# The opening of a hybrid decoder layer: x feature by token in three groups, rms by sums over partitions, gate sums moved into it

## The chip, the cores and the metric

One core of one Trainium2 chip. The metric is the device time of one execution in microseconds, the median of the runs; lower is better. A profile is one execution recorded by the hardware profiler.

## What is computed

One layer of a decoder on 1024 prompt tokens and 8 x 8 sample tokens (1088 tokens of 1024 features). The part that the change touches is the start: modulation by a condition, rmsnorm and the input projection.

```python
shift, scale, gate = jnp.split(jax.nn.silu(c) @ ada_w[l] + ada_b[l], 3, axis=-1)
h = rmsnorm(x, norm_w[l]) * (1.0 + scale[:, None, :]) + shift[:, None, :]
q_lat, kv_lat, k_pe, g_a, u, g_b, m_a, m_b = split_in(h @ w_in[l])
...
x = x + gate[:, None, :] * (merged @ w_out[l])

def rmsnorm(x, w):
    y = xf * lax.rsqrt(jnp.mean(xf * xf, axis=-1, keepdims=True) + EPS)
    return y.astype(x.dtype) * w
```

There is one condition for the prompt and one for each of the eight samples, so nine rows of shift, scale and gate. The rest (latent attention, a gated recurrence, two output projections, the final norm) is left as it is.

## The kernel before

All products are made of two parts: `split` (L53) casts a value to a high half on ACT (L55) and subtracts it on VectorE for the low half (L56); `mm3` (L76) issues three products, high x high, low x high and high x low (L79 to L81). The 1024 features lie in eight blocks (k) of 128 partitions; the tokens lie in three groups `GRP` of 364, 362 and 362 columns, of which the third ends with the 64 sample tokens.

The opening (L151 to L305) has these steps. `x_load` brings x in nine tiles of 128 tokens by 1024 features. `x_norm` (L220) squares a tile on ACT with a sum along its row, takes the power -0.5 on POOL (`rms_pow`, L109) and scales the tile on VectorE or POOL. `x_turn` (L231) turns it with eight transpositions on TensorE and copies it from PSUM to `xT`. `ada_load` (L184) brings block k of the shift and scale weights, 1 MB; `ada_sum` (L189) multiplies it by silu(c) on TensorE (eight fp32 products, in four strips of 32 partitions), and ACT copies the sum to `sa`; `ada_turn` (L199) transposes `sa` on TensorE, and VectorE adds the strips and writes block k of `aff`, the factors and shifts by feature. `h_part` (L241) applies them to the block on POOL (L245; the sample tokens on VectorE) and splits the result into `hh[k]` and `hl[k]`. `u_part` (L257) adds block k of the first two tiles of the u projection for one group: three products for each tile. The loop over k does for each block group 0 (six products), the turn of block k+1 and its `h_part` for all three groups, group 1, the sum of block k+2, and group 2.

Behind the opening comes `dense` (L372), the rest of the input projection: 26 tiles of 24 steps (`project`, L314, three products each), among which the sample attention and the recurrence are laid. Beside its tiles 2 to 17 runs `gate_sums` (L326): a load of 256 KB, four fp32 products with silu(c), and a VectorE copy or addition into `sgs`, which the end of the kernel reads as the gate.

TensorE's order is that of the program text (`manual_schedule` at L151). The other engines and SP's queue of DMAs get theirs from a planner, by the program's order as a priority, by when it takes an operand to be ready and by when a buffer of a pool comes free. Buffers of the opening's pool `p1`: three of `aw`; PSUM: four banks `pj`, two `pt` (both for the u sums) and two `px`.

Of the kernel before, what the change touches and what calls it, by code (L numbers as in the profile page):

```python
# [9 lines left out]
F32 = mybir.dt.float32  # L10
# [33 lines left out]
def trunk_step(ctx: ExitStack, tc: tile.TileContext, a, o):  # L44
# [76 lines left out]
    with ExitStack() as px_:  # L121
# [29 lines left out]
        with ExitStack() as pb, tc.manual_schedule(engines={mybir.EngineType.PE}):  # L151
# [30 lines left out]
            xT = p1.tile([P, KC, N], F32, name="xT", bufs=1)  # L182
# [6 lines left out]
            def ada_sum(aw):  # L189
# [5 lines left out]
                sa = p1.tile([P, 256], F32, name="sa")  # L195
# [13 lines left out]
            xs = {}  # L209

            def x_load(i):
                n = P if i < 8 else NS
                if i == 6:
                    xs[6] = p1.tile([P, KC, 256], F32, name="aw", bufs=3).rearrange("p a b -> p (a b)")
                    xs[6], xs[7] = xs[6][:, :D], xs[6][:, D:]
                elif i != 7:
                    xs[i] = p1.tile([P, D], F32, name="x", bufs=6)
                nc.sync.dma_start(xs[i][:n], a["xp"][i * P:(i + 1) * P] if i < 8 else a["xs"])

            def x_norm(i):  # L220

                n, x = P if i < 8 else NS, xs[i]
                st = p1.tile([P, 4], F32, name="st", bufs=4)
                S.activation(L[3][:n, :D], x[:n], AF.Square, accum_out=st[:n, 0:1])
                rms_pow(st[:n, 2:3], st[:n, 0:1], D, st[:n, 1:2])
                if i % 2:
                    G.tensor_scalar(x[:n], x[:n], st[:n, 2:3], 0.0, OP.mult, OP.add)
                else:
                    V.tensor_scalar(x[:n], x[:n], st[:n, 2:3], None, OP.mult)

            def x_turn(i):  # L231

                n, x = P if i < 8 else NS, xs[i]
                for j in range(2):
                    ps, tag = ((pt, "pt"), (pj, "pj"), (pj, "pj"))[(2 * i + j) % 3]
                    ps = ps.tile([P, 4, P], F32, name="pxt", tag=tag)
                    for k in range(4):
                        T.transpose(ps[:, k, :n], x[:n, (4 * j + k) * P:(4 * j + k + 1) * P], ident[:n, :n])
                    (S.copy if j == 0 and i % 2 == 0 else V.tensor_copy)(xT[:, 4 * j:4 * j + 4, i * P:i * P + n], ps[:, :, :n])

            def h_part(k, s, n):  # L241

                h = L[2 + k % 2][:, :N]
                m = min(s + n, NP)
                G.tensor_scalar(h[:, s:m], xT[:, k, s:m], aff[:, k, 1, 0:1], aff[:, k, 0, 0:1], OP.mult, OP.add)  # L245
                if s + n > NP:
                    h3 = hs[:, k].rearrange("p (b t) -> p b t", b=NB)
                    V.tensor_tensor(h3, xT[:, k, NP:].rearrange("p (b t) -> p b t", b=NB),
                                    aff[:, k, 1, 1:9].rearrange("p b -> p b ()").to_broadcast((P, NB, NT)), OP.mult)
                    V.tensor_tensor(h3, h3, aff[:, k, 0, 1:9].rearrange("p b -> p b ()").to_broadcast((P, NB, NT)),  # L250
                                    OP.add)
                    split(hh[k][:, NP:], hl[k][:, NP:], hs[:, k])
                split(hh[k][:, s:m], hl[k][:, s:m], h[:, s:m])
# [3 lines left out]
            def u_part(k, c, g):  # L257
                s, n = GRP[g]
                if k == 0:
                    pu[c, g] = (pj if g < 2 else pt).tile([P, 512], F32, name=f"pu{c}{g}", tag="pj" if g < 2 else "pt")  # L260
                mm3(pu[c, g][:, :n], [w[:, k, :] for w in u01[c]], [hh[k][:, s:s + n], hl[k][:, s:s + n]],
                    k == 0, k == KC - 1)

            for i in range(8):
                x_load(i)
            for i in range(9):
                x_norm(i)
                x_turn(i)
                if i == 0:
                    x_load(8)  # L270
                if i == 2:
                    aw = ada_load(0)
                if i == 3:
                    u01 = [weights(a["w_in"][c], (0,), (w_u0, None)[c]) for c in range(2)]
                    aw1 = ada_load(1)
                if i == 5:
                    sa = ada_sum(aw)
                if i == 6:
                    ada_turn(0, sa)
            aw = ada_load(2)  # L280
            h_part(0, *GRP[0])
            h_part(0, *GRP[1])
            h_part(0, *GRP[2])
            sa = ada_sum(aw1)
            for k in range(KC):
                if 0 < k and k + 2 < KC:
                    aw = ada_load(k + 2)
# [1131 lines left out]
```

## Time and profile before

| | us |
|---|---|
| median of 3 runs | 972.44 (972.28 to 972.62) |
| the profiled execution | 971.41 |
| its span, first to last instruction | 969.6 |
| busy: PE (TensorE matmul) | 936.1 (97%) |
| busy: DVE (VectorE) | 645.5 (67%) |
| busy: ACT (ScalarE) | 492.2 (51%) |
| busy: POOL (GpSimd) | 241.0 (25%) |

How to read the rows below. Times are us from the start of the span. A row of the timeline has start, duration, engine, line, operation, output and inputs, shapes, count (equal neighbours are merged into one row, from the first start to the last end) and in brackets how long the engine had been idle and what released it. PE is TensorE's products, PEld its weight loads. Matmuls are pipelined: their durations overlap, and the distance of two starts is what one costs. A row of the windows has the stretch, its length, the busy time of PE, PEld, DVE, ACT and POOL in it with the number of instructions, the granted TensorE clock (1.00 is 2.4 GHz), the share of the DMA engines, and GB/s. A row of the groups by form has line, engine, operation, tensors, shapes and count, then the busy time, the mean ns of one, and the idle time ahead of them. A row of one line's view has the shortest, median and longest duration in ns.

### The profile page before, as it was taken

To read this page: it belongs to the slowest core of one execution; us is meant where nothing else is said; L and a number is where in the kernel's file an instruction comes from. 1 tells how busy PE (TensorE), PEld (TensorE's weight loads), DVE (VectorE), ACT (ScalarE), POOL (GpSimd) and SP (SyncE) were. 2 spreads that over 40 slices of the span, in tenths; PEclk is the share of its full clock that TensorE was granted. 3 is DMA by queue.
4 is the path that set the end of the run, shared out by engine and by line. 5 is a ranking of instruction groups with operands and counts; after the bars stand their busy time and mean duration, and the time that the engine had idled before them with its cause. 6 is when DMAs were issued, how large, how long until landed. Compare 5 with 4: busy or idle time off the path is not lost. (4 is left out here: it accounts for less than half of the span.)

```text
span 969.6 us, 16493 instructions
## 1 busy us (share of the span) xinstructions
PE 936.1 (97%) x5933; PEld 860.2 (89%) x5933; DVE 645.5 (67%) x1518; ACT 492.2 (51%) x1150; POOL 241.0 (25%) x313
## 2 busy tenths in 40 slices
PE   5899999999999999999999999999999899999997
PEld 4677999999999999999999898888888799998886
DVE  5775664566666777766654367889889785880833
ACT  6447555544445444544443336777687664650311
POOL 5452210332222322222100034444445200000101
PEclk9999999999999999999999999999999999999999
DMA  9843132453443323333422213000011264741421
GB/s 337 287 142 110 49 108 94 146 152 109 141 129 125 113 77 120 103 110 119 117 78 97 65 53 69 12 7 22 7 34 34 69 198 155 246 140 35 152 87 66
DMA packets 52099, 104.62 MB, mean 108 GB/s; under 512 B 8177, under 2 KB 23601, under 8 KB 50994
## 3 DMA queue, kind: packets, MB, share of 16 engines
q1 hardware_dynamic: 46626, 84.69, 26.8%
q0 software_dynamic: 5392, 18.88, 6.6%
q8 instruction: 47, 0.77, 0.3%
q14 instruction: 34, 0.28, 0.1%
HBM read 85.58 MB, written 16.92 MB: 106 GB/s over the span
## 5 line engine op out<-in xcount | busy, mean ns | idle before, releaser
L79 PE MATMUL pj<-hh,whi 128*128 128x362 f32 (+2 forms) x656 | 223.9, 341 | 1.1 <-ACT L L145 1.1
L81 PE MATMUL pj<-hh,wlo 128*128 128x362 f32 (+2 forms) x656 | 217.1, 331 | 0.0
L80 PE MATMUL pj<-hl,whi 128*128 128x362 f32 (+2 forms) x656 | 216.8, 330 | 0.0
L79 PEld LDWEIGHTS pj<-hh,whi 128*128 128x128 f32 x656 | 123.5, 188 | 7.5 <-issue 4.7
L80 PEld LDWEIGHTS pj<-hl,whi 128*128 128x128 f32 x656 | 123.7, 189 | 1.7 <-issue 0.4
L81 PEld LDWEIGHTS pj<-hh,wlo 128*128 128x128 f32 x656 | 123.4, 188 | 1.7 <-issue 0.4
L644 POOL TENSOR_SCALAR nat<-raw 128x1024 fp32r<-128x1024 f32 x32 | 37.0, 1157 | 136.6 <-PE spo L65 81.6
L1038 POOL TENSOR_SCALAR pr<-pr,mx 128x128 f32<-128x128 f32 (+3 forms) x64 | 50.0, 782 | 83.2 <-DVE mx L1037 69.3
L1036 ACT ACTIVATE pr<-pr,mx 128x128 f32<-128x128 f32 (+3 forms) x64 | 49.8, 778 | 12.9 <-DVE mx L1034 12.6
L645 DVE TENSOR_TENSOR nat<-raw,nat 128x1024 fp32r<-128x1024 f32 x32 | 39.0, 1220 | 20.6 <-POOL nat L644 20.6
L641 POOL DMA_INDIRECT raw<-cache_ckv,idx x32 | 33.6, 1049 | 74.9 <-PE ptt L69 44.4
L1052 PE MATMUL ptr<-ident,pr 128*128 128x128 f32 x288 | 45.6, 276 | 4.1 <-DVE ptl L56 2.7
L112 POOL TENSOR_SCALAR ost<-ost 128x1 f32<-128x1 f32 (+1 forms) x9 | 2.9, 324 | 186.0 <-DVE ost L1296 186.0
L1293 ACT ACTIVATE ot<-xo 128x512 f32<-128x512 f32 (+2 forms) x19 | 11.5, 606 | 72.8 <-DVE xo L1292 68.5
L56 DVE TENSOR_TENSOR ptl<-ptr,pth 128x512 fp32r<-128x512 f32 (+1 forms) x80 | 45.7, 577 | 3.6 <-ACT pth L55 2.4
L694 ACT COPY stmp<-pss 64x512 f32<-64x512 f32 (+1 forms) x40 | 19.9, 497 | 55.0 <-PE pss L65 54.7
L56 DVE TENSOR_TENSOR wlo<-wraw,whi 128x512 fp32r<-128x512 f32 x58 | 39.4, 703 | 10.1 <-ACT whi L55 10.0
L55 ACT CAST pth<-ptr 128x512 fp32r<-128x512 f32 (+1 forms) x80 | 39.6, 499 | 9.7 <-PE ptr L1052 9.1
L56 DVE TENSOR_TENSOR tt<-ptt,tt 128x512 fp32r<-128x512 f32 x64 | 41.2, 679 | 4.8 <-ACT tt L55 4.4
L1052 PEld LDWEIGHTS ptr<-ident,pr 128*128 128x128 f32 x288 | 33.0, 140 | 12.6 <-DVE ptl L56 3.9
L55 ACT CAST whi<-wraw 128x512 fp32r<-128x512 f32 x58 | 34.0, 621 | 13.5 <-PE pj L80 13.4
L345 DVE COPY ev<-pj 128x364 f32<-128x364 f32 (+1 forms) x40 | 21.2, 530 | 29.4 <-PE pj L81 28.9
(472 smaller groups left out, 2588.5 us busy)
## 6 DMA issues: line engine op xcount, KB each, us to landing
wraw<-w_in SPq DMA_DIRECT2D x60, 256.0 KB, 3.2
sg<-g_dram SPq DMA_DIRECT2D x16, 544.0 KB, 3.6
aw<-ada_ss SPq DMA_DIRECT2D x8, 1024.0 KB, 7.2
g_dram<-ev SPq DMA_DIRECT2D x40, 181.0 KB, 2.4
wraw<-ada_g SPq DMA_DIRECT2D x16, 256.0 KB, 3.0
oraw<-w_out SPq DMA_DIRECT2D x16, 256.0 KB, 3.2
xo<-xp SPq DMA_DIRECT2D x8, 512.0 KB, 5.3
out_y<-xo SPq DMA_DIRECT2D x16, 256.0 KB, 2.1
```

The source lines that it names most:

```text
L55: S.copy(hi, src)
L56: V.tensor_tensor(lo, src, f(hi), OP.subtract)
L79: T.matmul(out, lhs[0], rhs[0], start=start, stop=False)
L80: T.matmul(out, lhs[0], rhs[1], start=False, stop=False)
L81: T.matmul(out, lhs[1], rhs[0], start=False, stop=stop)
L345: (S.copy if g == 1 else V.tensor_copy)(ev[:, :n], ps[:, :n])
L641: nc.gpsimd.indirect_dma_start(raw.rearrange("p k r -> p (k r)"), None, ckv_rows, bass.IndirectOffsetOnAxis(ap=idx[:, j, b:b + 1], axis=0))
L644: G.tensor_scalar(nat[:, 0], raw, 1.0, 0.0, OP.mult, OP.add)
L645: V.tensor_tensor(nat[:, 1], raw, f(nat[:, 0]), OP.subtract)
L1036: S.activation(pr[:, :w], pr[:, :w], AF.Exp, bias=mx[:, 1:2], scale=-1.0, accum_out=mx[:, 2:3])
L1038: G.tensor_scalar(pr[:, :w], pr[:, :w], mx[:, 3:4], 0.0, OP.mult, OP.add)
L1052: T.transpose(ps[:, k, i, :], pr[i][:, kc * P:(kc + 1) * P], ident)
```

## The change

x now comes transposed from the host, as three tensors of 128 partitions by 8 blocks by the group's tokens, two loads for each. The squares of a group are taken block by block on ACT and added on VectorE (`x_squares`); three narrow fp32 products with ones sum them over the partitions, so that a token lies on a partition, POOL takes the power, and VectorE writes three diagonal matrices (`x_rms`); one fp32 product with a 128 x 128 of ones spreads them, and ACT copies the result, R, one factor for each token on all partitions (`x_spread`). `h_part` multiplies a block by R on VectorE in place and then goes on as before; the sample tokens are done for all blocks at once (`h_sample`). The order of the opening is new: three blocks of group 0 first, then for each k the sum of block k+3, group 1 of block k, the turn of block k+3 and group 0 of block k+3; group 2 at the end. The gate's weights are laid out as four further blocks of 1 MB; their sums stand among the products of group 2 and are written by `ada_sum` to `sgs`, and `gate_sums` is gone from the dense loop.

```diff
-        G.tensor_tensor(out, tmp, nhalf[:n], OP.pow)
+        G.tensor_tensor(out, tmp, nhalf[:n].to_broadcast(tuple(out.shape)), OP.pow)
...
             def ada_load(k):
-                aw = p1.tile([P, KC, 256], F32, name="aw", bufs=3)
-                nc.sync.dma_start(aw, a["ada_ss"][k])
+                aw = p1.tile([P, KC, 256], F32, name="aw", bufs=4)
+                nc.sync.dma_start(aw, a["ada_ss"][k] if k < KC else a["ada_g"][k - KC])
                 return aw
...
+            def x_load(g):
                 for j in range(2):
+                    nc.sync.dma_start(xg[g][:, 4 * j:4 * j + 4], a[f"xT{g}"][:, 4 * j:4 * j + 4])
+
+            def x_squares(g):
+
+                n = GRP[g][1]
+                acc = p1.tile([P, 364], F32, name="acc", bufs=1)
+                S.activation(acc[:, :n], xg[g][:, 0], AF.Square)
+                for k in range(1, KC):
+                    sq = p1.tile([P, 364], F32, name="sq", bufs=2)
+                    S.activation(sq[:, :n], xg[g][:, k], AF.Square)
+                    V.tensor_tensor(acc[:, :n], acc[:, :n], sq[:, :n], OP.add)
+                return acc
+
+            def x_rms(g, acc):
...
+                for i in range(3):
+                    m = min(P, n - i * P)
+                    T.matmul(ps[:m, i:i + 1], acc[:, i * P:i * P + m], ones[:, 0:1], start=True, stop=True)
...
+                rms_pow(st[:, 4:7], st[:, 0:3], D, st[:, 0:3])
+                for i in range(3):
+                    V.tensor_scalar(rinv[:, i], ident, st[:, 4 + i:5 + i], None, OP.mult)
+
+            def x_spread(g):
+                n = GRP[g][1]
+                ps = px.tile([P, 512], F32, name="prb", tag="px")
+                T.matmul(ps[:, :n], ones, rinv.rearrange("p i t -> p (i t)")[:, :n], start=True, stop=True)
+                R[g] = p1.tile([P, 364], F32, name=f"R{g}", bufs=1)
+                S.copy(R[g][:, :n], ps[:, :n])
+
+            def h_part(k, g):
...
+                x = xg[g][:, k, :m - s]
+                V.tensor_tensor(x, x, R[g][:, :m - s], OP.mult)
+                G.tensor_scalar(h[:, s:m], x, aff[:, k, 1, 0:1], aff[:, k, 0, 0:1], OP.mult, OP.add)
+                split(hh[k][:, s:m], hl[k][:, s:m], h[:, s:m])
+
+            def h_sample():
+
+                m = NP - GRP[2][0]
+                V.tensor_tensor(hs, xg[2][:, :, m:], R[2][:, m:m + NS].rearrange("p t -> p () t").to_broadcast((P, KC, NS)),
+                                OP.mult)
+                h4 = hs.rearrange("p k (b t) -> p k b t", b=NB)
+                for j, op in ((1, OP.mult), (0, OP.add)):
+                    for k in range(0, KC, 4):
+                        V.tensor_tensor(h4[:, k:k + 4], h4[:, k:k + 4],
+                                        aff[:, k:k + 4, j, 1:9].rearrange("p k b -> p k b ()").to_broadcast((P, 4, NB, NT)),
+                                        op)
+                for k in range(KC):
                     split(hh[k][:, NP:], hl[k][:, NP:], hs[:, k])
...
+            x_load(0)
+            aw = {0: ada_load(0)}
+            u01 = [weights(a["w_in"][c], (0,), (w_u0, None)[c]) for c in range(2)]
+            aw[1] = ada_load(1)
+            x_load(1)
+            aw[2] = ada_load(2)
+            aw[3] = ada_load(3)
...
+            x_load(2)
+            sa = {0: ada_sum(aw[0])}
+            aw[4] = ada_load(4)
+            x_rms(0, x_squares(0))
+            ada_turn(0, sa[0])
+            x_spread(0)
+            h_part(0, 0)
+            sa[1] = ada_sum(aw[1])
+            aw[5] = ada_load(5)
+            u_part(0, 0)
+            ada_turn(1, sa[1])
+            h_part(1, 0)
+            acc1 = x_squares(1)
+            u_part(1, 0)
+            sa[2] = ada_sum(aw[2])
+            aw[6] = ada_load(6)
+            x_rms(1, acc1)
+            ada_turn(2, sa[2])
+            h_part(2, 0)
+            x_spread(1)
+            h_part(0, 1)
+            u_part(2, 0)
             for k in range(KC):
+                if k + 3 < KC:
+                    sa[k + 3] = ada_sum(aw[k + 3])
+                    if k + 7 < KC + 4:
+                        aw[k + 7] = ada_load(k + 7)
+                    if k == 1:
+                        acc2 = x_squares(2)
+                if k + 1 < KC:
+                    h_part(k + 1, 1)
+                u_part(k, 1)
+                if k + 3 < KC:
+                    ada_turn(k + 3, sa[k + 3])
+                    h_part(k + 3, 0)
+                    u_part(k + 3, 0)
+                if k == 2:
+                    x_rms(2, acc2)
                 if k == 3:
+                    x_spread(2)
                     w_u2 = weights(a["w_in"][2])
+                if k > 3:
+                    h_part(2 * k - 8, 2)
+                    h_part(2 * k - 7, 2)
+            h_sample()
+            for k in range(KC):
+                u_part(k, 2)
+                if k % 2:
+                    ada_sum(aw[KC + k // 2], sgs[:, 256 * (k // 2):256 * (k // 2) + 256])
+            nc.sync.dma_start(sgs[9:10], a["gate_b"])
...
-        def gate_sums(k, q):
-
-            aw = wp.tile([P, 512], F32, name="wraw", bufs=3)
-            nc.sync.dma_start(aw.rearrange("p (k j) -> p k j", k=4), a["ada_g"][k, :, 4 * q:4 * q + 4])
-            yield
-            ps = pj.tile([P, P], F32, name="pada", tag="pj")
-            for t in range(4):
-                mm(ps[32 * t:32 * t + 32, :], sc[:, 4 * q + t, :], aw[:, P * t:P * t + P], start=True, stop=True)
...
             def beside(n):
                 w[n + 1] = weights(a["w_in"][tiles[n + 1][0] if n + 1 < len(tiles) else 8])
-                m = n - 2
-                sums = gate_sums(m // 2, m % 2) if 0 <= m < 16 else iter(())
-                next(sums, None)
-                yield
-                next(sums, None)
                 yield
```

## Rows read from the trace of the kernel before

**Rows 1.** Windows, two stretches of the dense loop.
```profile
100.00:150.00 50.00, 50.00 (x324) 48.13 (x323) 29.54 (x39) 30.50 (x47) 10.31 (x9) 1.00 0.25 79
150.00:200.00 50.00, 48.29 (x305) 45.86 (x304) 27.38 (x53) 23.55 (x42) 9.89 (x11) 1.00 0.39 123
```

**Rows 2.** Timeline, TensorE: first transposition, first u product, first product of the dense loop.
```profile
9.04 6.99 PE L238 MATMUL pxt<-ident,x 128*128 128x128 f32 x32 [9.04 <-DVE x L229]
...
28.32 0.43 PE L79 MATMUL pu<-hh,wuh 128*128 128x364 f32 x1 [2.38 <-ACT hh L55]
...
66.41 0.43 PE L79 MATMUL pj<-hh,whi 128*128 128x364 f32 x1 [1.06 <-ACT L L145]
```

**Rows 3.** Timeline, TensorE, around one gate sum in the dense loop.
```profile
118.78 0.32 PE L80 MATMUL pj<-hl,whi 128*128 128x362 f32 x1
118.94 0.33 PE L81 MATMUL pj<-hh,wlo 128*128 128x362 f32 x1
119.20 0.42 PE L65 MATMUL pada<-wraw,sc 128*32 128x128 f32 x8
...
119.83 0.33 PE L80 MATMUL pj<-hl,whi 128*128 128x362 f32 x1
```

**Rows 4.** Timeline, all engines: from one turn to the cast of its block.
```profile
50.24 0.44 PE L202 MATMUL padt<-ident,sa 128*128 128x128 f32 x2
...
50.72 0.23 DVE L204 TENSOR_REDUCE ads<-padt 128x18 f32<-128x72 f32 x1 [0.30 <-PE padt L202]
...
51.13 0.28 DVE L206 TENSOR_SCALAR aff<-ads,bsc,vec 128x9 f32<-128x9 f32 x1
...
51.58 2.27 POOL L245 TENSOR_SCALAR L<-xT,aff 128x364 f32<-128x364 f32 x3 [2.14 <-DVE aff L206]
...
52.32 1.12 ACT L55 CAST hh<-L 128x364 fp32r<-128x364 f32 x2 [2.13 <-POOL L L245]
```

**Rows 5.** Timeline, TensorE's weight load of the second u product.
```profile
28.89 0.19 PEld L80 LDWEIGHTS pu<-hl,wuh 128*128 128x128 f32 x1 [0.39 <-DVE hl L56]
```

**Rows 6.** Timeline, TensorE, around one modulation sum of the opening.
```profile
51.34 0.33 PE L81 MATMUL pu<-hh,wlo 128*128 128x362 f32 x1
...
51.60 1.07 PE L194 MATMUL pada<-aw,sc 128*32 128x256 f32 x16
...
52.88 0.33 PE L80 MATMUL pu<-hl,wuh 128*128 128x362 f32 x1
```

**Rows 7.** Windows, the first 24 us.
```profile
0.00:24.00 24.00, 12.59 (x82) 10.02 (x82) 12.54 (x39) 16.76 (x29) 13.96 (x30) 1.00 0.93 338
```

**Rows 8.** Timeline, TensorE's weight loads of the first modulation sum.
```profile
19.27 0.59 PEld L194 LDWEIGHTS pada<-aw,sc 128*32 128x32 f32 x16 [0.26 <-DMA aw<-ada_ss]
```

**Rows 9.** Groups by form up to 66.4 us: the affine, the low half, the cast.
```profile
L245 POOL TENSOR_SCALAR L<-xT,aff 128x298 f32<-128x298 f32 x8 | 7.7, 958 | 0.0
...
L245 POOL TENSOR_SCALAR L<-xT,aff 128x364 f32<-128x364 f32 x8 | 5.5, 690 | 20.2 <-DVE aff L206 20.2
...
L56 DVE TENSOR_TENSOR hl<-L,hh 128x364 fp32r<-128x364 f32 x8 | 4.3, 535 | 5.9 <-ACT hh L55 5.9
...
L55 ACT CAST hh<-L 128x364 fp32r<-128x364 f32 x8 | 4.0, 496 | 17.0 <-POOL L L245 17.0
```

**Rows 10.** Timeline: the first norm, from POOL's first step to its reader.
```profile
7.24 0.19 POOL L112 TENSOR_SCALAR st<-st 128x1 f32<-128x1 f32 x1 [5.93 <-ACT L L224]
...
8.23 0.75 DVE L229 TENSOR_SCALAR x<-x,st 128x1024 f32<-128x1024 f32 x1 [1.13 <-POOL st L113]
```

**Rows 11.** One line's view: two fp32 products with ones, as four issues.
```profile
L938 PE MATMUL qss<-csr,ones x4: 592/594/595, 567.9 to 576.0; 128*128 128x512 f32 x4
```

**Rows 12.** Windows, around the first u products: the granted clock.
```profile
27.00:28.00 1.00, 0.00 (x0) 0.00 (x0) 0.90 (x2) 0.23 (x1) 0.91 (x2) 1.00 0.89 346
...
29.50:30.00 0.50, 0.50 (x3) 0.50 (x3) 0.50 (x3) 0.50 (x2) 0.00 (x0) 0.50 1.16 279
...
32.50:33.00 0.50, 0.50 (x10) 0.23 (x12) 0.50 (x2) 0.36 (x1) 0.50 (x2) 1.00 0.43 180
```

More of the change, by code (lines that the diff above doesn't have):

```diff
@@ L194, in ada_sum @@
                     T.matmul(ps[32 * t:32 * t + 32, :], sc[:, j, :], aw[:, j, :], start=j < 4, stop=j >= 4)
[L195 removed]
+                sa = p1.tile([P, 256], F32, name="sa") if sa is None else sa
                 S.copy(sa, ps)
@@ L231, in x_turn @@
-            def x_turn(i):
-                n, x = P if i < 8 else NS, xs[i]
-                for j in range(2):
[L235 to L239, printed above, removed]
@@ L252, in h_part, with u_part @@
                     split(hh[k][:, NP:], hl[k][:, NP:], hs[:, k])
-                split(hh[k][:, s:m], hl[k][:, s:m], h[:, s:m])
             pu = {}
-            def u_part(k, c, g):
+            def u_part(k, g):
                 s, n = GRP[g]
[L259 to L284, printed above, removed]
-            for k in range(KC):
-                if 0 < k and k + 2 < KC:
-                    aw = ada_load(k + 2)
-                if k == 0:
-                    for c in range(2):
-                        weights(a["w_in"][c], (1,), u01[c])
+                for c in range(2):
+                    if k == 0:
+                        pu[c, g] = (pj if g < 2 else pt).tile([P, 512], F32, name=f"pu{c}{g}",
+                                                             tag="pj" if g < 2 else "pt")
+                    mm3(pu[c, g][:, :n], [w[:, k, :] for w in u01[c]], [hh[k][:, s:s + n], hl[k][:, s:s + n]],
+                        k == 0, k == KC - 1)
@@ new lines, in trunk_step @@
+            x_load(0)
[5 more added lines that the diff above has]
+            aw[3] = ada_load(3)
+            for c in range(2):
+                weights(a["w_in"][c], (1,), u01[c])
+            x_load(2)
[3 more added lines that the diff above has]
+            ada_turn(0, sa[0])
@@ L291, in trunk_step @@
                 if k == 3:
+                    x_spread(2)
                     w_u2 = weights(a["w_in"][2])
-                for g in range(3):
-                    for c in range(2):
-                        u_part(k, c, g)
-                    if k + 1 < KC and g == 0:
-                        ada_turn(k + 1, sa)
-                        for j in range(3):
-                            h_part(k + 1, *GRP[j])
-                    if k + 2 < KC and g == 1:
-                        sa = ada_sum(aw)
+                if k > 3:
+                    h_part(2 * k - 8, 2)
+                    h_part(2 * k - 7, 2)
@@ L1326, in _layout @@
          "cache_ckv": c(i["cache_ckv"][0]), "cache_kpe": c(i["cache_kpe"][0])}
+    xT = np.concatenate([r["xp"], r["xs"]]).T.reshape(KC, P, N).transpose(1, 0, 2)
+    for g, (s, n) in enumerate(GRP):
+        r[f"xT{g}"] = c(xT[:, :, s:s + n])
     cT = np.zeros((P, KC, 32), np.float32)
```

51 lines of the change are left out of this document (15 added, 36 removed).

## The prediction

> **What bounds the kernel now.** I read the windows first. From 100 us on TensorE is busy in 50.00 of 50 us, and even the worse neighbour, 150 to 200 us, shows 48.29 [rows 1]: the long middle is bound by TensorE, so an instruction taken from TensorE there is worth its full price. The timeline of TensorE gives three marks of the opening [rows 2]: the first transposition starts at 9.04, the first product of the u projection at 28.32 after a wait of 2.38 us for the ACT cast of hh, and the first product of the dense loop at 66.41. Between 28.3 and 66.4 TensorE is fed: the products follow each other and the turns and sums of the modulation stand between them. So the change is worth two things: how far 66.41 moves, and what the gate sums cost in the dense loop. What comes after the dense loop is left as it is.
>
> **Gate sums leave the dense loop.** One gate sum is four fp32 products (eight issues). Products are 0.16 us apart (118.78, 118.94); without the sum the second product after 118.94 would start at 118.94 + 2 x 0.165 = 119.27, and it starts at 119.83 [rows 3]. So 0.56 us each, 16 of them, 9.0 us, all on the engine that sets the end. Their VectorE sums and 4.2 MB of loads leave the loop too, where neither is what TensorE waits for; I count nothing for them. Gain: -9.0.
>
> **The opening's new order.** TensorE's order is written by hand, and it decides. For k = 0 to 4 it is now: sum of block k+3, six products of group 1 (block k), turn of block k+3, six products of group 0 (block k+3). Before, 12 or more products stood between a turn and the first product that needs it. Now none does. The chain that a turn starts can be read off block by block [rows 4]: transposition at 50.24, VectorE reduce at 50.72, the scale at 51.13, POOL's affine at 51.58, the ACT cast from 52.32, about 0.50 long: 52.82, so 2.58 us from turn to the high half. The low half comes later: the second product of a block starts 0.57 us after the first (28.32, 28.89, waiting for VectorE's hl) where nothing is ahead [rows 2, 5]. Then five products at 0.165 follow, 0.83 us with the last one's start of the next: 2.58 + 0.57 + 0.83 + 0.07 = 4.05 us from a turn to the end of its products. The sum of the next block displaces 52.88 - 51.34 - 2 x 0.165 = 1.21 us [rows 6], and six products of group 1 take 1.0. One step takes 4.05 + 1.21 + 1.0 = 6.26 us, of which TensorE idles about 2.6. The wait sits on TensorE's own queue: everything written behind it waits too. The multiplication by R is ahead of the turn and costs the chain nothing.
>
> **What else goes and comes.** The 72 transpositions of x, their copies and the row-wise norm go; they lie ahead of 28.32, in the stretch whose marks are worked out anew below, so they have no price of their own. 24 squares (ACT), 21 additions and 24 multiplications (VectorE) come: they are in the marks where they end last, and elsewhere fill ACT and VectorE while TensorE waits for a chain; if that cover is gone, it is the group-2 wait below that grows. SP's queue gets four loads of 1 MB behind the modulation blocks: some 18.9 MB up to the last, 56 us at the rate of [rows 7], ahead of the gate sums that read them.
>
> **When the first of those turns comes.** Everything before it hangs on group 1's rms, since group 1's first products stand ahead of turn 3. Bytes queued up to the end of group 1's x: constants 0.33, x group 0 1.49, two modulation blocks 2.1, half of two u weights 0.52, x group 1 1.48: 5.9 MB. The mean over the first 24 us was 338 GB/s [rows 7], which gives 17.5 us. Before, modulation block 0 stood behind 5.8 to 6.4 MB and TensorE still waited for it at 19.27 [rows 8]; so I take 19 us for x and 22 us for block 2 (7.0 MB). Four squares of the second half are left then, 0.50 us each like the cast of that width, and one VectorE sum, 0.54 [rows 9]: 21.6. Sum 2 is written ahead of the rms products and lasts until 23.2. Then: three narrow products 0.5; two copies 0.4; the power on POOL, 0.99 from its first step to its reader (7.24 to 8.23) [rows 10]; three diagonals about 0.6; the spread, fp32 with a 128x128 of ones, which as two issues of 0.594 at 512 columns [rows 11] is about 0.75 at 362; a copy, a multiplication, the affine and a cast, 0.5 + 0.54 + 0.69 + 0.5, with 0.8 of hand-overs and queueing. That is 29.5 for the first group-1 product and 30.5 for turn 3. Group 0's products of blocks 0 to 2 are ready before it and gain nothing by being early: TensorE would only wait longer at group 1. Ends: 29 (22 us is block 2's own landing), 33 if the clock is low there (below).
>
> **Sum to the dense loop.** Turn 7: 30.5 + 4 x 6.26 + 1.25 for the rms and spread of group 2 = 56.8. Its products end at 60.85, three more blocks of group 1 at 63.85. Group 2 can only begin once R of group 2 is there: spread 2 stands behind block 6 of group 0, 53.8, plus 0.75 and a copy: 55.1. From there VectorE has eight multiplications and eight subtractions at about 0.5 (8.0), turn 7 and its low half (1.3), and ahead of the first group-2 product the sample's rows, five operations of 512 or 256 columns, 2.3 by the same rate per column: 66.7. POOL's affine took 0.958 us for 298 columns beside VectorE where 364 took 0.690 [rows 9], so the two get in each other's way; wholly one after the other (8 x 0.57 more) it is 71. If the planner pulled all of it forward, 63.85. I take 68, between the two prices that the rows give. Then 48 products, 8.0, and four gate sums, now as wide as the other sums, 4 x 1.21 = 4.85: the dense loop starts at 80.85 instead of 66.41, +14.4. The last gate sum covers the copies for which the loop's first product waited before; that is in the number.
>
> A rule that speaks against the change: the Trainium skill, SBUF — State Buffer, section "SBUF: two separate sides", says that VectorE operations with two SBUF inputs and POOL hold a shared port pair exclusively, the loser waiting for the whole instruction. The 0.958 against 0.690 agrees with it, but in one form; by the rule each turn's affine could lose a further 0.54 us, 2.7 in all, and the time would be 981.4. The sum goes without it.
>
> **Clock.** TensorE did nothing from 27 to 28 us (the end of the 2.38 us ahead of 28.32 [rows 2]); the granted clock, 1.00 then, was 0.50 (1.2 GHz) at 29.5 to 30 and back at 1.00 (2.4 GHz) in 32.5 to 33 [rows 12]. From 29.5 at the latest to 32.5 that is 3 us or a little more at half speed, which costs at most 1.7. The new waits (2.2 us at each turn, some four ahead of group 2) are of that kind, but in the loop half of TensorE's time is waiting anyway: between 0 and 8.5 for five turns, and I take 0.9.
>
> Total: -9.0 + 14.4 + 0.9 = +6.3. The profiled execution took 971.41 us (span 969.6), the median of the runs is 972.44, 1.03 more: 977.7 there, 978.7 as a median.
>
> **Rivals.** *The waits are filled* (the other side): if the planner reorders TensorE, or the chain is otherwise off its queue, a step is 3.66 (sum 1.21, turn 0.2, twelve products 2.0, some slack), turn 7 comes at 46.4, group 2 then waits for VectorE until about 59.6 (R at 44.7 plus the same work one after the other), and the dense loop starts at 72.4: +6.0 - 9.0, so 969.5. It decides once the chain is shorter than 2.58 by 6.3 / 5 = 1.3 us a turn. Against it: in the trace the sum at 51.60 and the products around it stand exactly as written; for it only that I haven't seen the new order run. *Group 2 is ready*: the planner fills VectorE's free half of each step with group 2, TensorE doesn't wait at 63.85: 978.7 - 4.15 - 0.9 = 973.7. Against it: R of group 2 comes at 55.1. *The clock falls at every turn*: 5 x 1.7 = 8.5 in place of 0.9: 986.3; the one fall in the trace followed 2.4 us of idling, each new wait has 2.2. *The removed sums were hidden*: then nothing is gained in the loop, 987.7; the windows with 50.00 of 50 us speak against it.
>
> **Chances.** Forecast 0.50 (974.5 to 984), waits filled 0.17, group 2 ready 0.14, clock at every turn 0.15, sums hidden 0.04. The range reaches from below the filled waits to above the clock's: 968 to 988. About 0.2% is what a measurement of this kernel can tell from no change (970.5 to 974.4): faster 0.19 (the filled waits, and a little of group 2 ready), same 0.14, slower 0.67.
>
> **What would show it.** Right: TensorE idle some 2 us behind each of turns 3 to 7, put down to the ACT cast of hh; a step near 6.3 us; a gap ahead of the first group-2 product put down to VectorE; the dense loop's first product near 81 us; no sums in the dense loop, and its windows full as now. Wrong: turn 3 much before 29, steps near 3.7, no gap ahead of group 2, or a dense loop that doesn't get shorter by about 9.

## The result, and the profile after

The changed kernel takes 1003.14 us (median of 4 runs, 1000.98 to 1003.59) against 972.36 (971.58 to 972.62): 1.0314 of the time, 95% interval 1.0296 to 1.0331. The direction was forecast, the size was not: 978.7, with a range up to 988.

The profiled execution took 1003.59 us (span 1001.8). The dense loop's first product stands at 105.53; in the kernel before it stands at 66.41 [rows 2], and 80.85 was forecast. From there to the end of the span it is 896.3 us instead of 903.2. So all of the loss lies ahead of the dense loop. Timeline of TensorE in the changed kernel (start, us, engine, line, operation; in brackets the wait before it and what ended it): three of group 0's first blocks, a sum, the rms products of group 1, turns 3 to 7 (L208), each with the first product of group 0 behind it, the first product of group 2, the dense loop:

```profile
22.70 0.67 PE L79 MATMUL pu<-hh,wuh 128*128 128x364 f32 x1 [1.48 <-ACT hh L55]
...
24.05 0.51 PE L79 MATMUL pu<-hh,whi 128*128 128x364 f32 x1
24.35 0.51 PE L80 MATMUL pu<-hl,whi 128*128 128x364 f32 x1
...
29.06 0.67 PE L79 MATMUL pu<-hh,wuh 128*128 128x364 f32 x1 [3.47 <-ACT hh L55]
...
31.45 1.75 PE L200 MATMUL pada<-aw,sc 128*32 128x256 f32 x16
33.13 0.79 PE L238 MATMUL pss__331<-ones,acc 128*128 128x1 f32 x6
...
38.73 0.67 PE L79 MATMUL pu<-hh,wuh 128*128 128x364 f32 x1 [0.95 <-ACT hh L55]
...
44.17 0.38 PE L208 MATMUL padt<-ident,sa 128*128 128x128 f32 x2
48.02 0.67 PE L79 MATMUL pu<-hh,wuh 128*128 128x364 f32 x1 [3.47 <-ACT hh L55]
...
53.86 0.38 PE L208 MATMUL padt<-ident,sa 128*128 128x128 f32 x2
56.29 0.43 PE L79 MATMUL pu<-hh,wuh 128*128 128x364 f32 x1 [2.06 <-ACT hh L55]
...
61.50 0.38 PE L208 MATMUL padt<-ident,sa 128*128 128x128 f32 x2
64.01 0.67 PE L79 MATMUL pu<-hh,wuh 128*128 128x364 f32 x1 [2.13 <-ACT hh L55]
...
70.88 0.38 PE L208 MATMUL padt<-ident,sa 128*128 128x128 f32 x2
73.39 0.43 PE L79 MATMUL pu<-hh,wuh 128*128 128x364 f32 x1 [2.14 <-ACT hh L55]
...
79.19 0.38 PE L208 MATMUL padt<-ident,sa 128*128 128x128 f32 x2
84.58 0.67 PE L79 MATMUL pu<-hh,wuh 128*128 128x364 f32 x1 [5.01 <-ACT hh L55]
...
92.80 0.43 PE L79 MATMUL pu<-hh,wuh 128*128 128x362 f32 x1 [0.79 <-ACT hh L55]
...
105.53 0.43 PE L79 MATMUL pj<-hh,whi 128*128 128x364 f32 x1
```

Two things are to be seen. The first product of every group-0 block waits for ACT's cast of hh. And turn 3, forecast for 30.5, comes at 44.17; the four steps from turn 3 to turn 7 take 35.02 us, where 26.3 was forecast (four times 6.26, and 1.25 for the norm of group 2). The waits of TensorE up to the dense loop (what waits, for what: us, times, longest) add up the first; for a load TensorE waits once only, ahead of its first sum:

```profile
PE pu L79 <- ACT hh L55: 21.5, 9, 5.0
PE pada L200 <- DMA aw<-ada_ss: 12.2, 1, 12.2
PE prb L250 <- DVE ads L210: 2.1, 1, 2.1
PE prb L250 <- DVE rinv L245: 1.8, 1, 1.8
```

The windows show the rest (length; busy us of PE, PEld, DVE, ACT, POOL; then granted clock, DMA share, GB/s). First five of the changed kernel's opening, then the whole opening from 8 us on, and a stretch of its dense loop:

```profile
20.00:28.00 8.00, 4.11 (x20) 2.32 (x12) 5.98 (x15) 3.08 (x7) 2.99 (x3) 1.00 1.02 419
...
36.00:44.00 8.00, 6.79 (x29) 3.74 (x30) 5.27 (x13) 3.61 (x9) 3.49 (x4) 0.57 0.17 70
...
52.00:60.00 8.00, 5.81 (x34) 3.90 (x30) 2.27 (x7) 1.36 (x3) 1.28 (x2) 0.71 0.38 131
60.00:68.00 8.00, 5.87 (x36) 4.69 (x32) 1.95 (x7) 1.36 (x3) 1.46 (x3) 0.71 0.37 131
...
92.00:100.00 8.00, 7.21 (x62) 5.52 (x62) 2.03 (x12) 2.01 (x10) 0.00 (x0) 1.00 0.03 8
...
8.00:105.53 97.53, 67.41 (x376) 45.17 (x376) 50.12 (x148) 33.15 (x82) 28.54 (x36) 0.83 0.49 188
...
150.00:200.00 50.00, 50.00 (x304) 49.93 (x303) 28.32 (x38) 31.05 (x45) 9.11 (x10) 1.00 0.26 83
```

The opening of the kernel before in the same view:

```profile
8.00:66.41 58.41, 50.46 (x360) 39.70 (x360) 41.04 (x114) 30.44 (x73) 33.09 (x52) 0.97 0.73 257
```

Before, TensorE had a mean clock of 0.97 ahead of the dense loop; now it is 0.83, with 0.57 to 0.71 from 36 to 76 us and 0.57 from 84 to 92. The 1.00 of 20 to 28 us does not fit the products, which start 0.30 us apart there (24.05, 24.35), where 0.165 is the distance at full speed [rows 3]; by that 0.83 is still too high. Behind turn 7 the half clock lasts until 90.81, shortly before group 2 (the distance of the products). VectorE's busy time went up, from 41.04 to 50.12 us. The dense loop itself is as full as before [rows 1].

### The profile page after: what moved, and what is told of

Read it like the earlier page. It is cut to its first block, busy times and chain, and to the rows that moved or that the text cites. A ratio compares the mean times of both kernels' runs of the same rounds, so it can differ in the third digit from the quotient of the medians.

```text
span 1001.8 us, 16279 instructions
## 1 busy us (share of the span) xinstructions
PE 944.6 (94%) x5821; PEld 862.7 (86%) x5821; DVE 649.3 (65%) x1538; ACT 492.8 (49%) x1158; POOL 230.7 (23%) x297
## 5 line engine op out<-in xcount | busy, mean ns | idle before, releaser
L671 POOL TENSOR_SCALAR nat<-raw 128x1024 fp32r<-128x1024 f32 x32 | 34.9, 1089 | 134.6 <-PE spo L65 66.7
L1063 ACT ACTIVATE pr<-pr,mx 128x128 f32<-128x128 f32 (+3 forms) x64 | 49.8, 778 | 12.8 <-DVE mx L1061 12.4
L81 PE MATMUL pout<-woh,mgl 128*128 128x512 f32 (+1 forms) x102 | 38.4, 377 | 0.0
```

The costliest lines, as they stand in the source:

```text
L81: T.matmul(out, lhs[1], rhs[0], start=False, stop=stop)
L671: G.tensor_scalar(nat[:, 0], raw, 1.0, 0.0, OP.mult, OP.add)
L1063: S.activation(pr[:, :w], pr[:, :w], AF.Exp, bias=mx[:, 1:2], scale=-1.0, accum_out=mx[:, 2:3])
```

## The experiments

Two marks carry most readings, both from TensorE's timeline: the dense loop's first product (D) and the time from D to the end of the span. A time without a number of runs is that of one execution. Where a kernel has several they lie 1 to 7 us apart, so a difference of 1 or 2 us between single ones is not read. In the changed kernel's profiled execution the first sum starts at 12.20, when its load has landed; in the runs built on it that is between 10.9 and 11.9. So some 1 us of what D gains on 105.53 (0.3 to 1.3) is this start and not the edit.

**e_open: the rebuilt opening alone.** The gate sums go back into the dense loop, in the kernel before's form.

```diff
-                if k % 2:
-                    ada_sum(aw[KC + k // 2], sgs[:, 256 * (k // 2):256 * (k // 2) + 256])
...
+                m = n - 2
+                sums = gate_sums(m // 2, m % 2) if 0 <= m < 16 else iter(())
+                next(sums, None)
```

> The rebuilt opening alone: the gate sums stay in the dense loop, as before the change, and the four sums among the products of group 2 go. If the two parts of the change add up, the dense loop's first product comes 4 x 1.21 = 4.9 us earlier than in the changed kernel (near 100.7 instead of 105.5) and the loop gets back what the sums cost there (6.9 to 9.0 us): 1005 to 1007 us. If the gate weights' four loads of 1 MB are what holds the opening up, the first product comes much earlier than that, and the time falls under 1000.

1008.73 us, 1.7 above the range of two parts that add up. D stands at 100.61, 4.92 ahead of the changed kernel's. From the first product of group 2 (92.34, and 92.80 there) to D it is 4.46 us less: the four wide sums that are no longer in front of it (4.85 forecast). So the loads of the gate's weights, gone here too, did not hold the opening up. From D to the end it is 906.4 us against 896.3: in the dense loop the sums cost 10.1 here, and 6.9 by the kernel before against the changed one. The forecast 9.0 lies between. The two differ because this dense stretch takes 3.2 us more than that of the kernel before with the same sums in it; why stays open. At D the opening alone is 34.2 us later than in the kernel before: all of the loss is its own.

**e_gates: the gate sums alone.** The old opening, with the four wide sums at its end.

```diff
-                sums = gate_sums(m // 2, m % 2) if 0 <= m < 16 else iter(())
...
+            for q in (2, 3):
+                ada_sum(ag[8 + q], sgs[:, 256 * q:256 * q + 256])
```

> The other part alone: the old opening, with the gate sums as four wide sums at its end (blocks 6 and 7 and behind them) and none in the dense loop. By the prediction's step the loop gains 9.0 (by what is left of the changed kernel's time behind its opening, 6.9) and the opening grows by 4.9, less the 1.06 us wait ahead of the dense loop that the last sum covers: 967.5 to 969.5 us. If the removed sums were hidden in the loop, 976. If their loads come too late at the end of the opening, 972 to 980.

975.6 us (10 runs, 971.66 to 978.34), 1.0024 of the kernel before (1.0009 to 1.0039): slower by a little, where 3 to 5 us of gain were expected. D is at 71.33, 4.92 later. That this is e_open's figure again is chance: 0.84 of it lie ahead of turn 7 and of the first of the four sums, and the last sum waits 1.59 us for its load, so the expectation's late loads are a part of it. From D to the end the profiled run takes 903.8, no less than before, and that is the larger part. From e_gates, two lines of TensorE's timeline, and windows at two places:

```profile
70.33 1.07 PE L194 MATMUL pada<-aw,sc 128*32 128x256 f32 x16 [1.59 <-DMA aw<-ada_g]
...
98.23 0.28 PE L69 MATMUL pqt<-ident,kvsq 64*128 64x64 f32 x1 [2.58 <-DVE kvsq L466]
```

```profile
100.00:105.00 5.00, 5.00 (x20) 2.50 (x19) 1.74 (x6) 1.00 (x2) 0.00 (x0) 0.74 0.17 56
...
530.00:535.00 5.00, 5.00 (x20) 5.00 (x20) 0.43 (x1) 1.23 (x5) 0.00 (x0) 0.50 0.11 27
535.00:540.00 5.00, 5.00 (x28) 5.00 (x28) 0.69 (x1) 0.98 (x2) 0.00 (x0) 0.89 0.23 76
```

Without the sums TensorE reaches two places of the dense stretch before VectorE and ACT are ready: it waits 2.58 us, and near 527 us 0.17, 0.44 and 0.29, and behind both the clock falls. In the kernel before the first of these waits is 0.58. The ten runs point the same way: the fastest (971.66) has a mean granted clock of 0.997, the slowest (978.34) 0.989.

**e_gates2: the same, with those two places mended.** More dense work goes ahead of the readers.

```diff
-                yield 7.0
+                yield 13.0
...
-                fill(3.0)
+                fill(6.0)
```

> The old opening with the gate sums at its end (as in e_gates, 975.6), and the two places mended where that run's TensorE waited in the dense stretch and then showed half clock: the products that read the sample's latent query come 6 us of dense work later (a wait of 2.58 us for VectorE), and 3 us more of dense work stand ahead of the puv products (waits of 0.17, 0.44 and 0.29). If these waits and the clock behind them are what ate the gain: first product of the dense loop at 71.3 as before, from it to the first puv product 449 to 452 instead of 455.3, from there to the end 445 instead of 448.5: 966 to 970, faster than the kernel before. If the gate sums were hidden in the dense loop, or other waits take their place: 973 to 976.

969.01 us (5 runs, 967.9 to 969.81) against 972.47: 0.9962 of the kernel before, 95% interval 0.9949 to 0.9976. It beats both kernels. From D (70.48) to the end it is 895.6, 8.2 less than in e_gates (6.6 by the medians of the whole time; the profiled one is the fastest of the five). Up to the second place, the first product into `puv`, it is 454.8 and from there 440.8. With the 3 us of dense work that the edit moved ahead of that product counted back it is 451.8 and 443.8, near the 449 to 452 and 445 that were expected. The same places in the timeline and the windows of e_gates2:

```profile
97.79 0.25 PE L69 MATMUL pqt<-ident,kvsq 64*128 64x64 f32 x1
```

```profile
100.00:105.00 5.00, 5.00 (x28) 3.39 (x27) 5.00 (x9) 3.98 (x8) 1.65 (x1) 1.00 0.32 97
...
530.00:535.00 5.00, 5.00 (x27) 4.47 (x26) 2.92 (x6) 2.00 (x4) 0.00 (x0) 1.00 0.41 117
535.00:540.00 5.00, 5.00 (x24) 4.14 (x23) 2.83 (x6) 3.52 (x8) 0.00 (x0) 1.00 0.63 172
```

Wait and fall are gone together. So here the removed sums were worth their price only once nothing that they covered came to light. The mending alone, on the kernel before, was not run; that kernel waits 0.58 and 0.17 us there, so little is to be had.

**e_order: group 0's products one turn later.**

```diff
                     h_part(k + 3, 0)
-                    u_part(k + 3, 0)
+                if 0 < k and k + 2 < KC:
+                    u_part(k + 2, 0)
```

> The changed kernel with one edit: group 0's products of a block are issued one turn later, so that between a turn and the first product that needs it stand six products of group 0, a sum, six products of group 1 and the next turn. Theory 'order' (the wait sits on TensorE's own queue behind each turn): the step from turn to turn falls from 8.8 us on average to 4 or 5, the opening by 16 to 20 us, 984 to 988 us, and the granted clock stays up in the loop. Rival 'clock' (what is slow is the half clock, whatever the order): the steps stay near 7 with TensorE busy at half speed, 994 to 1000 us. Rival 'port' (POOL's affine beside VectorE): the chain still takes 3.8 us but is covered, as with 'order'.

990.44 us, 2.4 above the range of 'order' and 3.6 below that of 'clock'; D at 92.74, 12.8 earlier. Turn 3 stands at 41.99 and turn 7 at 63.36 (TensorE's timeline), 5.34 a step. Of the waits behind the turns in the loop one is left, for block 7, and a new one came, for the copy of a sum that ACT does between squares and casts. Turns 4 and 7 and block 7's product in e_order's timeline of TensorE:

```profile
48.56 0.69 PE L208 MATMUL padt<-ident,sa 128*128 128x128 f32 x2 [4.00 <-ACT sa L202]
...
63.36 0.44 PE L208 MATMUL padt<-ident,sa 128*128 128x128 f32 x2 [0.16 <-ACT sa L202]
68.73 0.67 PE L79 MATMUL pu<-hh,wuh 128*128 128x364 f32 x1 [2.94 <-ACT hh L55]
```

The order of TensorE's queue is a cause, but not the whole one. That the clock would stay up did not come true: from 8 us to D its mean is 0.82.

**e_warm: the clock.** Unread transpositions of the identity fill the waits.

```diff
+            warm(50)
             sa = {0: ada_sum(aw[0])}
...
                     ada_turn(k + 3, sa[k + 3])
+                    warm(12)
```

> The changed kernel with extra transpositions of the identity whose results nobody reads: 50 ahead of sum 0, 12 behind each turn, 6 behind the spreads of groups 0 and 1, to fill TensorE's waits. 'Clock' (the half clock of the opening makes up most of the 24 us that the forecast missed): the granted clock reads 1.00 through the opening, sums take 1.1 instead of 1.9 us, and the dense loop starts 12 to 20 us earlier than 105.5: 983 to 991. 'Chain' (the waits for the ACT and VectorE chains set the opening, whatever TensorE's clock): the waits grow by what TensorE gets faster: 999 to 1003. 'Extra work' (the transpositions get in the way): above 1004.

992.58 us, 10.6 less than the changed kernel's median though TensorE does more: 1.6 above the range of 'clock', 6.4 below that of 'chain'. D is at 93.96, 11.6 earlier. Windows of this run, and from its timeline of TensorE turn 3, turn 4, the product behind that and turn 5:

```profile
36.00:44.00 8.00, 5.04 (x41) 3.64 (x41) 6.15 (x15) 3.75 (x10) 5.66 (x5) 1.00 0.36 133
...
52.00:60.00 8.00, 7.04 (x66) 5.34 (x66) 1.96 (x7) 1.43 (x4) 2.03 (x4) 1.00 0.52 197
60.00:68.00 8.00, 6.23 (x48) 4.62 (x48) 4.64 (x14) 3.22 (x7) 2.83 (x4) 1.00 0.83 248
```

```profile
40.06 0.38 PE L208 MATMUL padt<-ident,sa 128*128 128x128 f32 x2
...
47.97 0.38 PE L208 MATMUL padt<-ident,sa 128*128 128x128 f32 x2
...
50.41 0.43 PE L79 MATMUL pu<-hh,wuh 128*128 128x364 f32 x1 [0.75 <-ACT hh L55]
...
54.10 0.38 PE L208 MATMUL padt<-ident,sa 128*128 128x128 f32 x2
```

Behind turn 4 the chain, from the turn to the first product of its block, is 2.44 us and the step 6.13, where 2.58 and 6.26 were forecast. Behind turns 3, 5 and 6 the chain is 4.21, 2.51 and 3.33 us. The four steps take 28.42 us (turn 7 at 68.48), 6.6 less than in the changed kernel. Without the chains they take 15.93, which is what was forecast at full clock (15.97); in the changed kernel it is 23.72. Turn 3 still comes at 40.06: at most 4.1 us of its lateness is the clock, and 1.0 of these is the earlier start.

**e_early: the norm of group 1 earlier.** Its squares are issued behind spread 0, sum 2 and rms stand ahead of group 0's products of block 1 on TensorE, and spread 1 ahead of turn 2.

```diff
             x_spread(0)
+            acc1 = x_squares(1)
...
-            acc1 = x_squares(1)
-            u_part(1, 0)
             sa[2] = ada_sum(aw[2])
             aw[6] = ada_load(6)
             x_rms(1, acc1)
+            u_part(1, 0)
+            x_spread(1)
+            h_part(0, 1)
             ada_turn(2, sa[2])
             h_part(2, 0)
-            x_spread(1)
-            h_part(0, 1)
```

> The changed kernel with the squares of group 1 issued right behind spread 0, and sum 2, the rms products and spread 1 ahead of turn 2 on TensorE. 'Written order of the group-1 norm' (it stands behind the chain of turn 1): turn 3 comes at about 37 instead of 44.2, and the time is 994 to 998. 'Loads and ACT's amount of work' (the order is no limit): turn 3 stays at 42 to 46 and the time within 1001 to 1005.

1008.01 us, turn 3 at 45.93, D at 105.99: no gain and above both ranges, so as a cure the theory fell. The rms products came at 29.23, 3.9 earlier, after a wait of 3.07 us for VectorE's sum of the squares, but turn 2's chain then stood behind group 1's on VectorE. From the timeline of e_early, turn 2 on TensorE with its product, then VectorE's reduce and its scale:

```profile
34.27 0.44 PE L208 MATMUL padt<-ident,sa 128*128 128x128 f32 x2
...
40.71 0.67 PE L79 MATMUL pu<-hh,wuh 128*128 128x364 f32 x1 [6.00 <-ACT hh L55]
```

```profile
36.13 0.22 DVE L210 TENSOR_REDUCE ads<-padt 128x18 f32<-128x72 f32 x1
...
38.17 0.28 DVE L212 TENSOR_SCALAR aff<-ads,bsc,vec 128x9 f32<-128x9 f32 x1
```

VectorE runs multiplications, low halves and a weight split between the parts of the turn.

**e_act and e_fuse: POOL out of the chain.** In e_act ACT does the affine in POOL's place; in e_fuse VectorE multiplies by scale and R at once, and the shift goes into ACT's cast. Of the second, in excerpt:

```diff
-                V.tensor_tensor(x, x, R[g][:, :m - s], OP.mult)
-                G.tensor_scalar(h[:, s:m], x, aff[:, k, 1, 0:1], aff[:, k, 0, 0:1], OP.mult, OP.add)
...
+                V.scalar_tensor_tensor(h[:, s:m], x, aff[:, k, 1, 0:1], R[g][:, :m - s], OP.mult, OP.mult)
+                S.activation(hh[k][:, s:m], h[:, s:m], AF.Identity, bias=aff[:, k, 0, 0:1])
...
```

> The changed kernel with one edit: the affine of every block (factor and shift by feature) runs on ACT in place of POOL, so that the chain behind a turn has no POOL in it, nor anything that shares a port with VectorE's two-operand work. Theory 'port': the affine, now 1.58 to 1.74 us at blocks 0, 1 and 3 and queued behind others at block 7, takes 0.5 there; turn 3 comes 2 to 3 us earlier, the step of turn 3 is 1 us shorter, block 7's products come 2 to 3 us earlier: 995 to 998 us. 'Order' and 'clock' alone: at blocks 4, 5 and 6 the affine takes 0.67 on POOL already, so not more than 0.2 us each, 1001 us or more.

> The changed kernel with POOL out of the turn's chain: VectorE makes x times scale times R in one operation, ACT's cast adds the shift, VectorE's subtraction adds it again; all else as it was. 'POOL in the chain' (its affine, 0.69 alone and up to 1.74 beside VectorE, is a large part of the chains and keeps VectorE waiting at the shared port): a chain is 0.6 to 1.2 us shorter, turn 3 comes at 38 to 42 instead of 44.2, the dense loop starts 5 to 10 us earlier: 993 to 998. 'Clock and order' (POOL's part is small beside them): dense loop within 3 us of 105.5, 1000 to 1005.

e_act: 1004.81 us, D at 104.47. e_fuse: 1002.32, D at 101.66, turn 3 at 43.50. What POOL costs is there to be seen in the changed kernel, the affine of 364 columns beside VectorE and, at 36.90, alone (POOL's timeline):

```profile
20.54 1.58 POOL L262 TENSOR_SCALAR L<-xT,aff 128x364 f32<-128x364 f32 x1 [3.60 <-DVE xT L261]
...
26.75 1.74 POOL L262 TENSOR_SCALAR L<-xT,aff 128x364 f32<-128x364 f32 x1 [4.47 <-DVE aff L212]
...
36.90 0.65 POOL L262 TENSOR_SCALAR L<-xT,aff 128x364 f32<-128x364 f32 x1 [1.49 <-DVE aff L212]
```

At 36.90 VectorE is idle; from 26.54 on it runs two-operand work. But without POOL the opening is 1.1 or 3.9 us shorter, not 5 to 10, and 0.9 and 1.1 of that are the earlier start (first sum at 11.35 and 11.10), so the first can't be told from nothing. Neither time is clearly below the changed kernel's: both lie where 'clock and order' put them. At one place POOL did set the chain: behind turn 7 it is 3.06 us in e_act and 3.05 in e_fuse, against 5.39 in the changed kernel. In e_fuse the product still waits 2.05 to 2.72 us behind the turns of the loop. The line of TensorE's waits up to its dense loop:

```profile
PE pu L79 <- ACT hh L262: 16.8, 8, 2.7
```

**e_order_warm, e_all: the cures together.** The edits are those above; e_all has group 1's norm early too, squares, rms and spread of group 2 one block earlier, and 8 in place of 12 transpositions behind each turn.

> Both edits: group 0's products one turn later than their turn, and the extra transpositions (results unread). If order and clock are two separate losses: 12 us for the order as measured, and 8 to 16 more for the clock: 974 to 983. If the order had already removed the waits that make the clock fall, or the chain is what is left: 987 to 991.

> Order, the earlier norm of group 1, the extra transpositions (results unread) and squares, rms and spread of group 2 one block earlier, together. If the losses are the ones named and they add: the dense loop starts at 68 to 80 and the time is 965 to 977. If ACT and VectorE work bounds the opening once TensorE doesn't: 978 to 988.

986.7 us (D 89.33), 0.3 below the second reading, and 984.93 (4 runs, 983.78 to 986.64; 1.0129 of the kernel before, 1.0111 to 1.0146; D 87.42), in the second range. The gains do not add: 12.7 and 10.6 alone, 16.4 together, 18.2 with all four. So the two cures share a part of their gain; which part, these runs don't show. In e_order_warm a wait of 5.09 us for ACT's cast is left ahead of group 2.

**e_best, e_best2: a third form of the opening.** TensorE sums the squares itself, in 8 products a group with a matrix of 1/1024; ACT's square root and VectorE's reciprocal follow; POOL is out; TensorE's order is written anew, twice.

```diff
+                    T.matmul(XS[g][:, :n], ones, sq[:, :n], start=k == 0, stop=k == KC - 1)
...
+                    S.activation(R[g][:, :n], XS[g][:, :n], AF.Sqrt, bias=epst)
+                    V.reciprocal(R[g][:, :n], R[g][:, :n])
```

> The opening with every loss that the runs have named taken out: group 0's products one turn later; the squares summed over partitions and blocks by TensorE itself (24 products with a matrix of 1/1024, which keep it busy and replace VectorE's additions, the rms products and the spread); rms by ACT's square root and VectorE's reciprocal; POOL out of the chain as in the run beside it; gate sums ahead of group 2 and inside it; 40 extra transpositions ahead of sum 0 whose results nobody reads. If waits, clock and VectorE's work were what made the opening long: dense loop at 66 to 78, 959 to 973. If the loads or ACT bound it once these are gone: dense loop at 80 to 90, 974 to 986.

> The run before (e_best) with TensorE's order alone changed, by its three long waits: sum 2, turn 2 and group 0's products of block 2 ahead of the first product of group 1 (a wait of 4.38 us there), the squares of group 2 one and a half blocks earlier so that their reciprocal doesn't stand ahead of turn 7 (3.83), gate sums 0 and 1 where turn 7's chain runs; and 70 in place of 40 unread transpositions ahead of sum 0. If the order of work is what is left: the dense loop's first product at 68 to 74 instead of 79.5, 966 to 974. If VectorE's amount of work bounds the opening: 76 to 80, 977 to 983.

982.26 us (4 runs, 980.34 to 983.19; 1.0108, 1.0091 to 1.0125; D 79.45) and 978.78 (6 runs, 974.95 to 979.48; 1.0059, 1.0042 to 1.0076; D 75.99). The time of the first lies in its second range, its D between the two. The better one is still slower than the kernel before, and its time and D lie where 'VectorE's amount of work' put them (D to 0.01). A window of e_best2 ahead of its group 2, and one of its three reciprocals in VectorE's timeline:

```profile
48.00:68.00 20.00, 16.05 (x149) 10.58 (x147) 19.95 (x46) 11.26 (x27) 0.79 (x1) 1.00 0.68 231
```

```profile
48.41 2.42 DVE L234 RECIPROCAL R<-R 128x362 f32<-128x362 f32 x1
```

In this stretch TensorE has its full clock, and VectorE is busy 19.95 of 20 us: its amount of work is the bound here. From 8 us to D VectorE has 44.89 us of it, the kernel before 41.04; 7.3 of the 44.89 are the three reciprocals, which neither of the other two kernels has in its norm. Ahead of 48 us this opening is not free of waits and of the low clock: its mean is 0.84 from 8 to 28 us and 0.91 from 28 to 48.

## Why the prediction was right or wrong

The profiled run is 25.9 us above the forecast for one (1003.6 against 977.7). By its steps: turn 3 comes 13.7 later; the four steps to turn 7 take 8.7 more, 35.0 instead of 26.3; from turn 7 to the end of group 1's products it is 5.6 more, 12.7 instead of 7.1; ahead of group 2 the wait is 3.2 less; the tail is as forecast to 0.1. That makes 24.7 at D. The dense loop gave 2.1 less than 9.0, and 0.9 had been set aside for the clock: 25.9.

*The gate sums.* Right behind the new opening: 6.9 and 10.1 by two pairs of traces, 9.0 forecast. Behind the old one they first gave nothing (903.8 against 903.2). What the step left out is what the sums covered: with the old opening, taking them away uncovered a wait of 2.58 us and two falls of the clock, and the gain only came (e_gates2) when these places were mended.

*The chain and the step.* The chain was right for turns 4 to 6: 2.43, 2.51 and 2.51 us in the changed kernel, 2.58 forecast; behind turn 3 it was 3.85. The step was right as arithmetic at full clock (e_warm). The rival of filled waits was priced too well: e_order's step is 5.34 where 3.66 stood, with one wait of 4.00 in it, and the time was 990.4, not 969.5.

*The clock.* This term failed: 0.9 forecast, 10.6 by e_warm (up to 1 us of it the earlier start). The failing sentence is that in the loop half of TensorE's time is waiting anyway. Turn, products and sum stand in series with the chain that follows them, so what they lose at half speed is added to the step; the waiting doesn't absorb it, it comes after. Of the 8.7 us that the four steps took more, the chains are 1.0, and 7.7 are TensorE's own work, 23.7 us instead of 16.0. By e_warm the clock's 11.6 at D are 4.1 ahead of turn 3 (1.0 of it the start), 6.6 in the four steps and 0.9 behind turn 7. I had looked for single falls of 3 us; the rows of the changed kernel show 0.57 to 0.71 for tens of microseconds, since each step has a new wait and the clock does not come back for good before the next. The kernel before had 72 transpositions of x in its opening, and 0.97. The rival of a fall at every turn had the right kind and, with 8.5, most of the size; the stretch ahead of turn 3 was not in it.

*When turn 3 comes.* The largest miss, and no rival held it. The step that failed is that group 0's products of blocks 0 to 2 are ready before group 1's rms and so cost nothing. Each waited for ACT's cast of its block: 1.48, 3.47 and 0.95 us. The product of block 1 stands ahead of sum 2 and of the rms products on TensorE's queue, so that sum 2 began at 31.45 and ended at 33.13, where 23.2 was forecast for its end; and the squares of group 1 on ACT alternate with VectorE's additions, which stand among turns and low halves and end at 31.56, where 21.6 was forecast. These two come 1.6 us apart, so that a cure of either alone could gain little. The loads were not late: in 0 to 24 us they ran at 362 GB/s where the forecast took 338, and the first square of group 1 starts at 22.55 without a wait for one. Turn 2, block 2's products and sum 3 then stand ahead of group 1 too. Of 13.7 us the clock is 3.1 to 4.1 (e_warm); the rest is these chains. Moving that norm forward did not mend it (e_early), since on VectorE the chain of the next turn then comes late. How that rest divides among queue order, VectorE and ACT, no run settles.

*Turn 7 to the end of group 1.* Block 7's chain took 5.39 us (79.19 to 84.58), 2.8 more than forecast: POOL and VectorE were in group 2's work by then, which the forecast had counted on VectorE without letting it delay this chain. With POOL out it is 3.06 and 3.05 (e_act, e_fuse), so POOL's queue is most of it. The other 2.8 is 24 products, 20 of them 0.30 instead of 0.165 us apart.

*Ahead of group 2.* The wait of 4.15 us for VectorE did not come, only 0.79 us for ACT's cast: group 1's products ended so late (near 91.85, where 63.85 was forecast) that group 2's work was nearly done. Here the rival of a ready group 2 was nearer, for another reason than its own.

*POOL beside VectorE.* The rule of the Trainium skill (SBUF — State Buffer, section "SBUF: two separate sides") agrees with the affine of 1.58 to 1.74 us beside two-operand work and 0.65 alone. But taking POOL out gained 1.1 and 3.9 us at D, some 1 us of each by the earlier start, where 2.7 was priced by that rule; it does not explain the miss.

*What was not in the sum at all.* The rebuilt opening gives VectorE more work: 21 additions and 24 multiplications come, and it is busy 50.12 us up to D against 41.04. I counted them as cover. e_best2 shows VectorE's work as the bound of a stretch of 20 us, but with another norm; that it would be the changed kernel's next bound is argued from the 50.12, not shown.

## What to carry to other kernels

The waits put into TensorE's queue cost twice here: the wait, and the half clock of what stands in series behind it (23.7 us for 16.0 in four steps). Price such a loop at both clocks, and read from a trace which one it gets. Before an instruction is taken from a full engine, look for what it was covering: the next reader along the queue may not be ready, and giving that reader a few us more of filler was the difference between slower (1.0024) and faster (0.9962) here. When an opening is rebuilt, add up the busy time of every engine before and after; an engine whose total grows is a candidate for the next bound even if it was idle enough before.

## What the runs showed of the hardware

- The clock column reads 1.00 for the first stretches of the changed kernel, while its products start 0.30 us apart (24.05, 24.35, 24.65). In e_order the same products start 0.17 us apart (22.61, 22.78, 22.95). The spacing of like instructions told the clock there, and the column did not.
- Unread transpositions hold the clock: in e_warm the column reads 1.00 from 20 to 68 us, and sums take 1.07 us where the first seven of the changed kernel take 1.75 to 1.94. Behind turn 7, where a wait of 2.99 us was left after them, products were 0.30 us apart again (from 74.26 to 77.28).
- Waits of 0.17, 0.44 and 0.29 us among short products of 128 columns (e_gates, 527.1 to 529.7) were followed by five microseconds at 0.50 (530 to 535).
- VectorE's reciprocal took 2.42 us for 362 columns, where its two-operand operations of that width take 0.53 (the changed kernel) to 0.60 (e_best2).
